# Moving both ends of on-chip memory: 256 bytes more at the left end, 384 more at the right end

## The chip, the cores and the metric

The kernel runs on one core of one Trainium2 chip. The metric is device time in microseconds (us) of one execution. A core has five engines that run their own instruction streams: TensorE (PE in the profile; its weight loads are listed apart as PEld), VectorE (DVE), ScalarE (ACT), GpSimd (POOL) and SyncE (SP, which here issues nearly all DMAs). They share the on-chip memory SBUF, 128 partitions wide; an address below is a byte address within a partition. TensorE reads two operands from it: the weights of a matmul (`lhsT`, 128 columns, loaded by an instruction of their own, LDWEIGHTS) and the moving operand (`rhs`, here mostly 512 columns of 4 bytes), and writes to PSUM.

## The reference, cut to what matters

One layer of a streaming encoder on x of shape (1, 2048, 1024), in float32:

```python
h = rmsnorm(x, mix_norm_g)
q, k, v, u, vg = split(h @ w_in)                 # 1024 -> 2560
a = band_attention(q, k, v, ...)                 # 8 heads x 64, chunks of 64, 8 chunks back
g = gelu(u) * spatial(rmsnorm(gelu(vg)))         # per group a 128x128 mix over positions
x = x + concat(rmsnorm(a), rmsnorm(g)) @ w_out   # 1024 -> 1024
h = rmsnorm(x, ffn_norm_g)
gate, up = split(h @ w_ffn_in)                   # 1024 -> 2 x 2816
x = x + (silu(gate) * up) @ w_ffn_out            # 2816 -> 1024
```

## The kernel before, in words

The large products keep float32 accuracy by splitting each operand into a rounded part (type float32r) and the rest; `split` (lines 80 to 82) makes them, ACT the first and DVE the second, and `mm3` (lines 84 to 87) runs three matmuls for one product: high times high, high times low, low times high. So lines 85, 86 and 87 carry nearly all TensorE work, in four stages:

1. Projections (`project`, line 272): 80 units of 8 x 3 matmuls of 128x512. `xh`, `xl` are the weights of the array (pool `xs`), `wh`, `wl` move (pool `ws`). Between them stand the small mix of the gating group (`pm`, line 329) and, in the second half, the attention of the first four tiles.
2. Attention of the other tiles (lines 160 to 210) with pieces of the output projection (`out_piece`, line 548) between the heads: one piece is one `mm3`, `mh`, `ml` as weights and `woh`, `wol` moving. The order of TensorE in this stage is written out by hand.
3. The first FFN product, by a seven-product scheme (Strassen-Winograd) on 2x2 blocks: `block` (line 715) runs seven products of 12 matmuls, 84 in all; 44 blocks, 22 in each half of the positions. Product number o reads the moving tiles `ys[o]` (made by `prep`, line 678, from `y_d`) and weights out of the pool `wi3` (made by `weights`, line 691). Line 671 puts the pools of `ys[5]` and `ys[6]` on the right side of memory; `ys[0]` to `ys[4]` are on the left.
4. The second FFN product, by the same scheme (`product`, line 803): 77 groups of 8 x 3 matmuls, `ah`, `al` (pool `at4`) as weights and `oh`, `ol` (pool `wt4`) moving.

Outside stage 2 a planner orders the instructions by a simulated time. Each engine then runs its list in order and waits on semaphores.

Memory is handed out from two ends. A pool on the left side starts where the pools below it end, a pool on the right side ends where those above it start, so the size of the first tile at an end moves every pool of that side. On the left come 16384 bytes that the runtime keeps, 128 bytes of built-in constants and the pool `consts` (line 46: `ident` and `identr` 512 bytes each, `nhalf` and `g1` 32, `rx` 64); the next pool starts at byte 17664. On the right, under the top of memory at 229376, come 32 bytes and the tile `edge` (line 48: 24 floats, 96 bytes), which nothing uses; the pool below ends at 229248. With the sizes of the pools between, the tiles that TensorE reads start at these addresses modulo 512 (each tile or slice that a 128x512 matmul reads is a multiple of 512 bytes from the next):

| stage | weights | side, mod 512 | moving | side, mod 512 |
|---|---|---|---|---|
| 1 | `xh`, `xl` | right, 0 | `wh`, `wl` | right, 0 |
| 1, mix | `wsh`, `wsl` | left, 288 | `vh`, `vl`, four strided slices of 64 | left, 256 or 0 |
| 2 | `mh`, `ml` | left, 256 | `woh`, `wol` | left, 256 |
| 2 | `qd` | right, 128 | `kTw` | right, 128 and 384 |
| 2, transposes | `pr` | right, 384 | `ident` | left, 128 |
| 3 | `wih`, `wil` | right, 384 | `ys[0]` to `ys[4]` | left, 256 |
| 3 | `wih`, `wil` | right, 384 | `ys[5]`, `ys[6]` | right, 384 |
| 4 | `ah`, `al` | left, 256 | `oh`, `ol` | right, 384 |

Of the kernel before, what the change touches and what calls it, by code (L numbers as in the profile page):

```python
# [8 lines left out]
F32 = mybir.dt.float32  # L9
# [9 lines left out]
P = 128  # L19
# [23 lines left out]
def block_kernel(ctx: ExitStack, tc: tile.TileContext, x, xT, w_in, mixg, qg, kg, bias, sgug, wsT, bsp, outg, w_out, ffng, w_fi, w_fo, out):  # L43
    nc = tc.nc

    consts = ctx.enter_context(tc.tile_pool(name="consts", bufs=1))
    edge = ctx.enter_context(tc.tile_pool(name="edge", bufs=1, side="right"))
    edge.tile([P, 24], F32, name="edge")
    dram = ctx.enter_context(tc.tile_pool(name="dram", bufs=1, space=DRAM))

    kT_d = dram.tile([P, H, SEQ], F32, name="kT_d")
# [837 lines left out]
```

## Time and profile before

| | |
|---|---|
| median of 3 runs | 2252.26 us (2251.11 to 2253.65) |
| profiled execution | 2248.34 us, its span 2246.6 us |
| granted clock of TensorE, mean | 0.998 |
| PE busy | 2200.9 us, 98% |
| PEld busy | 1810.0 us, 81% |
| DVE, ACT, POOL busy | 56%, 41%, 41% |
| DMA queue q1, share of 16 engines | 48.0% |

Rows below come from one profiled execution. The span runs from its first to its last instruction. A matmul's record lasts longer than the distance to the next start, since matmuls are pipelined: the rate is read from the starts, or from the number of records in a stretch, not from the duration. A `bank<-yh,wih` is a matmul into the PSUM tile `bank` from the tiles `yh` and `wih`.

### The profile page before, as it was taken

Reading aid. Unit: us, or ns where it says so; the run is one execution under the profiler, and the core shown is the slowest. Engines: PE = TensorE matmul, PEld = TensorE weight load, DVE = VectorE, ACT = ScalarE, POOL = GpSimd, SP = SyncE. Lnnn points to the kernel's source line nnn. Section 1 sums busy time; section 2 is a strip of 40 time slices with the busy share of each in tenths; the row PEclk is TensorE's granted clock in tenths of the full one; section 3 lists DMA queues with packets and bytes.
Section 4 is the critical chain, followed back from the end, with each engine's and each line's share of the span. In section 5 each row is a group of like instructions: output and inputs, shape, how many; then the busy total and the mean of one; then the engine's idle time right before and its main releaser. Section 6 shows DMA issues by size and latency. Waiting matters only on the chain.

```text
span 2246.6 us, 33040 instructions
## 1 busy us (share of the span) xinstructions
PE 2200.9 (98%) x12648; PEld 1810.0 (81%) x12648; DVE 1268.4 (56%) x1799; ACT 911.8 (41%) x1663; POOL 915.8 (41%) x789
## 2 busy tenths in 40 slices
PE   8999999999999999799999998999999999999999
PEld 7888888887888888688888886788888878888787
DVE  3366345774666666775555558565555533544555
ACT  6434544554555555443333335333332323222322
POOL 1254114320011100756566665665656412603434
PEclk9999999999999999999999999999999999999999
DMA  7244616558878873932323236232323263733463
GB/s 259 76 131 135 221 66 191 166 168 295 252 226 265 265 234 131 298 118 90 122 89 120 82 131 194 89 121 89 113 89 113 95 234 134 283 117 119 151 229 133
DMA packets 183805, 361.37 MB, mean 161 GB/s; under 512 B 15328, under 2 KB 68576, under 8 KB 182112
## 3 DMA queue, kind: packets, MB, share of 16 engines
q1 hardware_dynamic: 183504, 359.27, 48.0%
q8 instruction: 99, 1.62, 0.3%
q14 instruction: 58, 0.48, 0.1%
q10 hardware_dynamic: 144, 0.00, 0.0%
HBM read 256.45 MB, written 102.76 MB: 160 GB/s over the span
## 4 chain that ended last, share of the span: by engine, by line
PE 82%; DVE 4%; POOL 4%; DMA 4%; issue 3%; ACT 2%; SPq 1%; POOLq 0%; DVEq 0%; ACTq 0%
PE bank L85 17%; PE bank L86 17%; PE bank L87 17%; PE ps L85 6%; PE ps L86 6%; PE ps L87 6%; PE pv L210 2%; PE S L171 2%; PE pt L198 2%; PE po L85 2%; PE po L87 2%; PE po L86 2%; DMA kTw<-kT_d 1%; DMA ynat<-y_d 1%; POOL g L723 1%
## 5 line engine op out<-in xcount | busy, mean ns | idle before, releaser
L86 PE MATMUL bank<-yl,wih 128*128 128x512 f32 x1232 | 486.5, 395 | 4.0 <-DVE yl L82 4.0
L85 PE MATMUL bank<-yh,wih 128*128 128x512 f32 x1232 | 483.4, 395 | 7.0 <-ACT wih L81 5.0
L87 PE MATMUL bank<-yh,wil 128*128 128x512 f32 x1232 | 482.4, 394 | 0.0
L85 PEld LDWEIGHTS bank<-yh,wih 128*128 128x128 f32 x1232 | 232.2, 189 | 63.5 <-ACT wih L81 5.4
L86 PEld LDWEIGHTS bank<-yl,wih 128*128 128x128 f32 x1232 | 232.1, 188 | 60.7 <-DVE yl L82 7.1
L87 PEld LDWEIGHTS bank<-yh,wil 128*128 128x128 f32 x1232 | 232.0, 188 | 53.8
L85 PE MATMUL ps<-wh,xh 128*128 128x512 f32 x640 | 251.7, 398 | 7.9 <-ACT wh L81 7.9
L86 PE MATMUL ps<-wl,xh 128*128 128x512 f32 x640 | 250.2, 392 | 1.7 <-DVE wl L82 1.7
L87 PE MATMUL ps<-wh,xl 128*128 128x512 f32 x640 | 250.4, 391 | 0.0
L86 PE MATMUL bank<-ol,ah 128*128 128x512 f32 x616 | 243.1, 395 | 0.0
L85 PE MATMUL bank<-oh,ah 128*128 128x512 f32 x616 | 240.8, 395 | 1.0 <-ACT oh L81 1.0
L82 DVE TENSOR_TENSOR al<-ar,ah 128x1024 fp32r<-128x1024 f32 x77 | 109.5, 1421 | 212.8 <-ACT ah L81 212.7
L87 PE MATMUL bank<-oh,al 128*128 128x512 f32 x616 | 224.5, 395 | 1.7 <-DVE al L82 1.7
L82 DVE TENSOR_TENSOR wil<-s,wih 128x512 fp32r<-128x512 f32 x176 | 172.6, 1013 | 76.5 <-ACT wih L81 76.3
L81 ACT CAST ah<-ar 128x1024 fp32r<-128x1024 f32 x77 | 80.8, 1049 | 301.7 <-PE bank L86 281.2
L723 POOL TENSOR_TENSOR g<-up,g 128x512 f32<-128x512 f32 x88 | 138.6, 1576 | 82.2 <-DVE up L722 82.2
L81 ACT CAST wih<-s 128x512 fp32r<-128x512 f32 x176 | 101.5, 617 | 169.2 <-POOL s L700 116.1
L85 PEld LDWEIGHTS ps<-wh,xh 128*128 128x128 f32 x640 | 120.6, 189 | 31.0 <-ACT wh L81 7.9
L81 ACT CAST wih<-wir 128x512 fp32r<-128x512 f32 x132 | 81.5, 617 | 157.7 <-PE bank L86 144.9
L86 PEld LDWEIGHTS ps<-wl,xh 128*128 128x128 f32 x640 | 120.6, 188 | 25.9 <-DVE wl L82 2.5
L87 PEld LDWEIGHTS ps<-wh,xl 128*128 128x128 f32 x640 | 120.4, 188 | 25.0
L87 PEld LDWEIGHTS bank<-oh,al 128*128 128x128 f32 x616 | 116.0, 188 | 29.2 <-DVE al L82 2.2
(175 smaller groups left out, 4092.7 us busy)
## 6 DMA issues: line engine op xcount, KB each, us to landing
wir<-in_w_fi SPq DMA_DIRECT2D x88, 512.0 KB, 3.3
ar<-f_d SPq DMA_DIRECT2D x77, 512.0 KB, 3.3
kTw<-kT_d SPq DMA_DIRECT2D x96, 320.0 KB, 4.1
f_d<-g SPq DMA_DIRECT2D x22, 1024.0 KB, 4.2
wr<-in_w_in SPq DMA_DIRECT2D x40, 512.0 KB, 5.0
f_d<-c SPq DMA_DIRECT2D x22, 768.0 KB, 4.5
wor<-in_w_fo SPq DMA_DIRECT2D x66, 256.0 KB, 3.7
ynat<-y_d SPq DMA_DIRECT2D x56, 256.0 KB, 4.6
```

The costliest lines, as they stand in the source:

```text
L81: nc.scalar.copy(hi, src)
L82: nc.vector.tensor_sub(lo, src, hi.bitcast(F32))
L85: nc.tensor.matmul(ps, lhsT=lh, rhs=rh, start=first, stop=False)
L86: nc.tensor.matmul(ps, lhsT=lh, rhs=rl, start=False, stop=False)
L87: nc.tensor.matmul(ps, lhsT=ll, rhs=rh, start=False, stop=last)
L171: nc.tensor.matmul(S[:, i, :hw], lhsT=q[:, p], rhs=k[:, i * hw : (i + 1) * hw], start=p == 0, stop=p == 1)
L198: nc.tensor.transpose(pt[:, i], pr[:, i * P : (i + 1) * P], ident)
L210: nc.tensor.matmul(o, lhsT=a[:, i], rhs=vt[m + 1 - nk + i][:, c, h * HD : (h + 1) * HD], start=n == 0, stop=n == len(seq) - 1)
L723: nc.gpsimd.tensor_tensor(g[:, i], t, g[:, i], op=ALU.mult)
```

## The change

The tile `edge` at the right end grows from 24 to 120 floats (96 to 480 bytes), and a tile `skip` of 64 floats (256 bytes) is added to the pool `consts`, ahead of `ident`. Nothing reads or writes either. All tiles behind `skip` on the left lie 256 bytes higher, all pools on the right 384 bytes lower; with the 32 bytes above it `edge` now fills 512 bytes, and the left pools start at byte 17920, which is 35 x 512.

```diff
     consts = ctx.enter_context(tc.tile_pool(name="consts", bufs=1))
     edge = ctx.enter_context(tc.tile_pool(name="edge", bufs=1, side="right"))
-    edge.tile([P, 24], F32, name="edge")
+    edge.tile([P, 120], F32, name="edge")
+    consts.tile([P, 64], F32, name="skip")
     dram = ctx.enter_context(tc.tile_pool(name="dram", bufs=1, space=DRAM))
```

## Rows read from the trace of the kernel before

**Rows 1.** The page: busy us of each engine; the chain's shares by engine.

```profile
PE 2200.9 (98%) x12648; PEld 1810.0 (81%) x12648; DVE 1268.4 (56%) x1799; ACT 911.8 (41%) x1663; POOL 915.8 (41%) x789
...
PE 82%; DVE 4%; POOL 4%; DMA 4%; issue 3%; ACT 2%; SPq 1%; POOLq 0%; DVEq 0%; ACTq 0%
```

**Rows 2.** Windows by stage: us; PE, PEld, DVE, ACT, POOL busy (count); clock; DMA.

```profile
0.00:630.00 630.00, 612.49 (x3864) 513.81 (x3865) 346.33 (x591) 315.82 (x599) 158.65 (x244) 1.00 0.56 180
...
929.00:1803.40 874.40, 858.74 (x3681) 692.34 (x3681) 513.35 (x617) 307.02 (x513) 544.37 (x372) 0.99 0.34 118
1803.40:2241.60 438.20, 435.46 (x1873) 352.35 (x1871) 212.93 (x203) 126.34 (x166) 158.13 (x102) 1.00 0.49 173
```

**Rows 3.** Windows, PE alone, tile ps (projections): us, busy (count), clock, DMA.

```profile
215.00:315.00 100.00, 100.00 (x443) 1.00 0.46 163
```

**Rows 4.** Windows, PE alone, tile bank: the two FFN stages.

```profile
1095.00:1365.00 270.00, 270.00 (x1167) 1.00 0.33 113
...
1860.00:2120.00 260.00, 260.00 (x1121) 1.00 0.45 158
```

**Rows 5.** Groups by line and form, 1095:1365 and 1860:2120: busy, mean | idle, releaser.

```profile
L81 ACT CAST wih<-wir 128x512 fp32r<-128x512 f32 x42 | 25.9, 618 | 55.6 <-PE bank L86 55.6
...
L81 ACT CAST ah<-ar 128x1024 fp32r<-128x1024 f32 x47 | 49.3, 1049 | 179.8 <-PE bank L86 167.6 <-DMA ar<-f_d 11.3 <-PE bank L87 0.9
```

**Rows 6.** Timeline of PE in one block of stage 3: start us, us, what.

```profile
1178.08 0.40 PE L87 MATMUL bank<-yh,wil 128*128 128x512 f32 x1
...
1188.12 0.39 PE L85 MATMUL bank<-yh,wih 128*128 128x512 f32 x1
...
1190.91 0.39 PE L85 MATMUL bank<-yh,wih 128*128 128x512 f32 x1
...
1193.18 0.39 PE L86 MATMUL bank<-yl,wih 128*128 128x512 f32 x1
```

**Rows 7.** Timeline of PE: output projection at the end of stage 2.

```profile
917.50 0.39 PE L86 MATMUL po<-wol,mh 128*128 128x512 f32 x1
...
925.20 0.39 PE L87 MATMUL po<-woh,ml 128*128 128x512 f32 x1
```

**Rows 8.** Windows, PE alone: the two long stretches of stage 3.

```profile
953.00:1323.80 370.80, 370.80 (x1601) 1.00 0.30 105
...
1437.30:1803.40 366.10, 366.07 (x1580) 1.00 0.29 105
```

**Rows 9.** Chain of waits, change of halves, first and last: start us, us, what.

```profile
1323.85 0.69 DVE u L737
...
1437.33 0.50 PE bank L85
```

**Rows 10.** Chain of waits at the start of stage 3.

```profile
947.19 1.94 PE pth L572 x8
...
950.64 0.43 PE bank L85
```

**Rows 11.** Timeline of PE in stage 2: a piece's end, then a transpose.

```profile
682.23 0.39 PE L87 MATMUL po<-woh,ml 128*128 128x512 f32 x1
682.46 0.27 PE L195 MATMUL S<-ident,pr 128*128 128x128 f32 x1
```

**Rows 12.** Groups by line and form, 1095:1365: POOL.

```profile
L723 POOL TENSOR_TENSOR g<-up,g 128x512 f32<-128x512 f32 x27 | 42.5, 1576 | 22.5 <-DVE up L722 22.5
...
L735 POOL TENSOR_TENSOR v<-v,u 128x512 f32<-128x512 f32 x14 | 22.1, 1576 | 11.6 <-ACT v L734 11.6
```

**Rows 13.** The page's DMA issues: out<-in, count, KB each, us to landing.

```profile
wir<-in_w_fi SPq DMA_DIRECT2D x88, 512.0 KB, 3.3
ar<-f_d SPq DMA_DIRECT2D x77, 512.0 KB, 3.3
```

**Rows 14.** Timeline of PE: the gating group's mix in stage 1.

```profile
83.49 0.28 PE L86 MATMUL pm<-vl,wsh 128*128 128x256 f32 x1
...
84.32 0.28 PE L87 MATMUL pm<-vh,wsl 128*128 128x256 f32 x1
```

## The prediction

> **What bounds the kernel now.** I read the busy line first: TensorE is busy 98% of the span, no other engine above 56%, and the chain that ended last lies on PE for 82% [rows 1]. A busy PE may still run below its own best rate, so the stages come next, by the windows [rows 2]: the projections (0 to 630 us), the FFN's first products (929 to 1803) and its second ones (1803 to 2242); the attention with the output projection lies between 630 and 929. PE is busy 97 to 99% of the three, so the time of a stage is its number of matmuls times the distance between two starts. That distance is what I compare from stage to stage. A window counts each record that overlaps it; a 512-column record lasts 0.39 to 0.40 us and starts are 0.23 us apart, so 1.7 of the count began before the window.
>
> Projections: 100 us with 443 - 1.7 records, 226.6 ns from start to start [rows 3]. First FFN products: 270 / (1167 - 1.7) = 231.7 ns; second ones: 260 / (1121 - 1.7) = 232.3 ns [rows 4]. All three run at granted clock 1.00 and with no PE idle time, with the same shape and type. The slower two aren't short of operands either: the casts that make them, on ACT, wait for PE to give buffers back (55.6 of 55.6 us for `wih<-wir`, 167.6 of 179.8 for `ah<-ar`) [rows 5].
>
> What differs is where the operands lie. By the table of residues in the section on the kernel before, `ws` and `xs` agree modulo 512 (both 0), `oh` and `ah` don't (384, 256), and in the first FFN products two of seven pairs agree: `ys[5]` and `ys[6]`, on the right like the weights at 384; `ys[0]` to `ys[4]` are at 256. One block of 84 matmuls shows both: from 1178.08 us 43 starts take 10.04 us, 233.5 ns each, in the products with `ys[1]` to `ys[4]`; at its end, in those with the right-hand tiles, ten starts take 2.27 us, 227 ns [rows 6]. Output projections at the end of the attention, left with left, both 256: 34 starts in 7.70 us, 226.5 ns [rows 7]. So pairs at 0/0, 256/256 and 384/384 run at 226.5 to 227 ns (I take 226.7), pairs that differ by 128 or 384 at about 232 to 233.
>
> **The change part by part.** No instruction is added or removed; two tiles that nobody uses move every other address. Left tiles go up by 256 bytes, right ones down by 384, which is +128 modulo 512.
>
> Second FFN products: 256 and 384 both become 0. 616 x 3 = 1848 matmuls x (232.3 - 226.7) = 10.3 us. PE is on the chain there throughout, and ACT and DVE wait for it.
>
> First FFN products: 256 + 256 and 384 + 128 both become 0, so the five unmatched pairs match and the two matched ones stay so. The saving is 231.7 - 226.7 = 5.0 ns per matmul, averaged over the seven products, but only where PE sets the time. From 953 to 1323.8 us and from 1437.3 to 1803.4 us it does: 1601 + 1580 - 3.4 = 3178 matmuls [rows 8], 15.9 us. Between the two, as the halves change, the chain runs for 113 us through DVE, POOL and the loads of `ynat`, and comes back to PE at 1437.33 [rows 9]; a faster PE waits longer there, and I count nothing. At the start the chain runs through the transposes that wait for `h` until 947 us [rows 10]; nothing there either.
>
> Projections: 0/0 become 128/128. No row has a 512-column pair at 128. The bound from one side is nothing, from the other the price of an unmatched pair, 640 x 3 x 5.0 = 9.6 us. The nearest rows are the three equal pairs, all alike, so I take nothing.
>
> Attention: `woh` and `mh` stay equal, and `kTw` and `qd` both move by 128. What changes is the neighbour across the sides: where a right-hand weight load runs behind an output projection, as at 682.23 us, the spacing is 230 ns here [rows 11]. 256 + 256 + 256 such matmuls x up to 5 ns make -3.8 to +3.8 us; a gain is likelier, since the first transposes' weights (384 against 256) would then agree with `woh`. I take 0.5 us.
>
> Other engines: POOL's product of a left and a right tile (256, 384; L723) takes 1576 ns, that of two left ones (256, 256; L735) 1576 ns [rows 12], so agreement is worth nothing to it. DMA: `wir` lands at residue 384, `ar` at 256, both 512 KB in 3.3 us [rows 13]. Nothing again; the bound is the landing time of a few loads at the change of halves, 1 us either way. [...]
>
> Sum: 10.3 + 15.9 + 0.5 = 26.7 us, of which I take 26, since the first groups of a stage lag. Against the profiled execution (2248.34 us: the span of 2246.6 and 1.7 around it) that is 2222. The median of the runs shown is 3.9 us above that execution, so I set it against the median: 2252.3 - 26 = 2226 us.
>
> [...] Matched matmuls run at 226.7 ns here [rows 3, 7]. [...]
>
> **The rivals.** *Sides, not residues: no change.* Every matched 512-column pair in the trace also lies on one side of memory, and nearly every slow one has an operand on each. If the side decides, moving both ends does nothing: 2252 us. For it: no row shows a pair across the sides at equal residue. Against it: the mix `pm`, left with left at 288 against 256 or 0, takes 0.83 us for 7 matmuls of 256 columns, 118.6 ns [rows 14], where half of 226.7 is 113.4; but its moving operand is strided, so this is weak. [...] Chance 0.07.
>
> *Slower: the side decides, and the projections fall out of step.* Then the FFN gains nothing, and the pair at 128/128 is not like 0/0; at the unmatched price the projections pay 1920 x 5.0 = 9.6 us: 2262 us. It decides as soon as more than about 5 us is lost there without the FFN's gain. For it: 128 is the one residue that no row shows for a 512-column pair. Against it: 0, 256 and 384 alike. Chance 0.05.
>
> *Part of it.* If the other stage boundaries swallow more (PE ahead of the weights' preparation, the projections losing their 9.6 us while the FFN gains), 10 to 17 us remain: 2235 to 2242 us. Against it: ACT waits for PE in both FFN stages [rows 5]. Chance 0.10.
>
> **How the numbers follow.** Forecast 0.78: 2220 to 2232 us, from 20 to 32 us saved (26, with 3.8 of the attention and 2 of the clock either way). With the near half of the third rival the range is 2219 to 2237 us. About 0.2% (4.5 us) is what a measurement of this kernel can tell from no change. Faster: 0.78 + 0.10 = 0.88; the same 0.07; slower 0.05.
>
> **What would show it.** In the changed kernel the same windows should count: first FFN products 270 / 0.2267 + 1.7 = 1193 records in 270 us for 1167, second ones 1149 in 260 us for 1121, projections still 443 in 100 us. All seven products of a block should show 227 ns, a block 84 x 226.7 ns = 19.04 us for 84 x 231.7 = 19.46. The 113 us at the change of halves should stay as long, with up to 2 us more of waiting in it. The prediction is wrong if the FFN windows still count 1167 and 1121 (the sides decide), or if the projections' count falls.

## The result and the profile after

The changed kernel takes 2228.53 us (median of 4 runs, 2227.2 to 2230.03) against 2252.22 us of the kernel before on the same chip (4 runs): a ratio of 0.9895 [0.9878, 0.9912], 23.7 us less. Two more sets of the same kernel gave 0.9896 and 0.9901 (below). The forecast was 2226 us in a range of 2219 to 2237.

The profiled execution took 2228.25 us, its span 2226.5. It holds the same 12648 matmuls in the same order; the line numbers are one higher (L86 to L88 are `mm3`). First the page of the changed kernel, the lines that answer to [rows 1]:

```profile
PE 2177.4 (98%) x12648; PEld 1811.7 (81%) x12648; DVE 1277.8 (57%) x1799; ACT 911.2 (41%) x1663; POOL 910.6 (41%) x789
...
PE 79%; DMA 5%; DVE 5%; POOL 4%; issue 4%; ACT 2%; SPq 1%; DVEq 0%; POOLq 0%; ACTq 0%
```

PE's busy time falls by 23.5 us and its share of the span stays at 98%: the engine that set the time still does, and does the same list faster. Where, the windows by stage tell (columns as in [rows 2]; stages 1 and 2 in one):

```profile
0.00:934.40 934.40, 909.84 (x7096) 768.39 (x7097) 542.11 (x980) 478.54 (x985) 211.81 (x315) 1.00 0.61 194
934.40:1793.10 858.70, 842.45 (x3681) 692.23 (x3680) 520.46 (x617) 306.17 (x513) 542.25 (x372) 0.99 0.35 120
1793.10:2221.80 428.70, 425.06 (x1873) 351.05 (x1871) 214.35 (x204) 126.54 (x166) 156.53 (x102) 1.00 0.51 177
```

Stage 3 takes 858.7 us for 874.4, stage 4 428.7 for 438.2, with the same counts of matmuls. Stages 1 and 2 end at 934.4 for 929: 5.4 us later in this execution, which comes back below. The spacing within the two FFN stages, PE alone, tile `bank`, answers to [rows 4]:

```profile
1095.00:1365.00 270.00, 270.00 (x1193) 1.00 0.34 117
1860.00:2080.00 220.00, 220.00 (x972) 1.00 0.48 166
```

270 / (1193 - 1.7) = 226.6 ns for 231.7, and 220 / (972 - 1.7) = 226.7 ns for 232.3: 26 more matmuls in the same 270 us, at the same granted clock and with PE never idle. The timeline of PE in one block of stage 3, in the products with left-hand tiles that ran at 233.5 ns in [rows 6]:

```profile
1180.20 0.39 PE L87 MATMUL bank<-yl,wih 128*128 128x512 f32 x1
...
1185.64 0.39 PE L87 MATMUL bank<-yl,wih 128*128 128x512 f32 x1
```

24 starts in 5.44 us, 226.7 ns: as fast as the right-hand tiles were before. A whole block takes 19.04 us for 19.45. The projections' window, tile `ps`, answers to [rows 3]:

```profile
215.00:315.00 100.00, 99.71 (x440) 1.00 0.48 167
```

440 records for 443, in 0.3 us less of busy time; from start to start 226.9 ns for 226.7: the pair at 128/128 runs as the one at 0/0 did. The 5.4 us of stages 1 and 2 show in the waits of PE before 934.4 us (us in total, times, longest), of which the first two are absent before:

```profile
PE Ss L179 <- DMA qe<-qe_d: 2.7, 1, 2.7
PE S L172 <- DMA kTw<-kT_d: 2.5, 1, 2.5
```

Two loads of the attention came late, and behind the wait for `qe` the granted clock was 0.57 from 368 to 372 us. In two other executions with the same addresses stage 3 begins at 929.64 and 930.11 us, so the 5.4 us are not lost in every execution. But a wait for one of these loads or for both, of 0.4 to 2.8 us each, stands in all 13 profiles with moved addresses and not in the one before. Whether the moved addresses have a share in it stays open, with one profile of before.

### The profile page after: what moved, and what is told of

Its sections match the earlier page's. It is cut to its first block, busy times and chain, and to the rows that moved or that the text cites. A ratio compares the mean times of both kernels' runs of the same rounds, so it can differ in the third digit from the quotient of the medians.

```text
span 2226.5 us, 33040 instructions
## 1 busy us (share of the span) xinstructions
PE 2177.4 (98%) x12648; PEld 1811.7 (81%) x12648; DVE 1277.8 (57%) x1799; ACT 911.2 (41%) x1663; POOL 910.6 (41%) x789
## 4 chain that ended last, share of the span: by engine, by line
PE 79%; DMA 5%; DVE 5%; POOL 4%; issue 4%; ACT 2%; SPq 1%; DVEq 0%; POOLq 0%; ACTq 0%
PE bank L86 16%; PE bank L88 16%; PE bank L87 16%; PE ps L86 5%; PE ps L87 5%; PE ps L88 5%; PE pv L211 2%; PE S L172 2%; PE pt L199 2%; PE po L86 2%; PE po L87 2%; PE po L88 2%; DMA kTw<-kT_d 1%; DVE wil L83 1%; POOL g L724 1%
## 5 line engine op out<-in xcount | busy, mean ns | idle before, releaser
L86 PE MATMUL bank<-yh,wih 128*128 128x512 f32 x1232 | 478.8, 391 | 7.7 <-DVE g L719 3.1
L87 PE MATMUL bank<-yl,wih 128*128 128x512 f32 x1232 | 481.8, 391 | 4.0 <-DVE yl L83 3.9
L88 PE MATMUL bank<-yh,wil 128*128 128x512 f32 x1232 | 477.5, 390 | 0.0
L86 PEld LDWEIGHTS bank<-yh,wih 128*128 128x128 f32 x1232 | 232.1, 188 | 59.1 <-DVE g L719 4.6
L87 PEld LDWEIGHTS bank<-yl,wih 128*128 128x128 f32 x1232 | 232.1, 188 | 55.1 <-DVE yl L83 7.3
L88 PEld LDWEIGHTS bank<-yh,wil 128*128 128x128 f32 x1232 | 232.2, 188 | 48.2
L86 PE MATMUL ps<-wh,xh 128*128 128x512 f32 x640 | 252.9, 400 | 7.8 <-ACT wh L82 7.8
L87 PE MATMUL ps<-wl,xh 128*128 128x512 f32 x640 | 251.5, 394 | 1.7 <-DVE wl L83 1.7
L88 PE MATMUL ps<-wh,xl 128*128 128x512 f32 x640 | 252.0, 394 | 0.0
L87 PE MATMUL bank<-ol,ah 128*128 128x512 f32 x616 | 239.8, 389 | 0.0
L86 PE MATMUL bank<-oh,ah 128*128 128x512 f32 x616 | 237.5, 389 | 1.6 <-ACT oh L82 1.6
L83 DVE TENSOR_TENSOR wil<-s,wih 128x512 fp32r<-128x512 f32 x176 | 177.8, 1048 | 85.8 <-ACT wih L82 85.7
L88 PE MATMUL bank<-oh,al 128*128 128x512 f32 x616 | 221.2, 389 | 2.1 <-DVE al L83 2.1
L86 PEld LDWEIGHTS ps<-wh,xh 128*128 128x128 f32 x640 | 121.3, 190 | 31.0 <-ACT wh L82 7.8
L87 PEld LDWEIGHTS ps<-wl,xh 128*128 128x128 f32 x640 | 121.4, 190 | 26.0 <-DVE wl L83 2.6
L88 PEld LDWEIGHTS ps<-wh,xl 128*128 128x128 f32 x640 | 121.2, 189 | 25.2
L700 POOL TENSOR_TENSOR s<-wir 128x512 f32<-128x512 f32 x44 | 59.9, 1360 | 189.8 <-DMA wir<-in_w_fi 179.9
```

What stands on the lines that cost most here:

```text
L83: nc.vector.tensor_sub(lo, src, hi.bitcast(F32))
L86: nc.tensor.matmul(ps, lhsT=lh, rhs=rh, start=first, stop=False)
L87: nc.tensor.matmul(ps, lhsT=lh, rhs=rl, start=False, stop=False)
L88: nc.tensor.matmul(ps, lhsT=ll, rhs=rh, start=False, stop=last)
L700: nc.gpsimd.tensor_add(s1, x21, x22)
```

## The experiments

Unless a diff says otherwise, an experiment starts from the changed kernel. "Difference" is the byte address of the moving operand less that of the weights, modulo 512.

**One end, by 128 bytes.** The left end moves by 128, the right stays as before. All FFN pairs then agree at 384/384, none at 0.

```diff
-    edge.tile([P, 120], F32, name="edge")
-    consts.tile([P, 64], F32, name="skip")
+    edge.tile([P, 24], F32, name="edge")
+    consts.tile([P, 32], F32, name="skip")
```

> The change with one end alone and without a multiple of 512: the left end moves up by 128 bytes, the right end stays. Left tiles come to 384 modulo 512, as the right ones of both FFN stages are; the projections keep 0/0. Theory (the pair must agree modulo 512): stage 3 counts 1192 records of tile bank in 270 us (226.7 ns), a block takes 19.04 us, stage 4 1148 in 260 us; time 2226 to 2231 us, as the changed kernel or up to 2 us below it. Rival A (both operands must lie at multiples of 512): 231.7 and 232.3 ns as before, 2250 to 2254 us. Rival B (the sides decide): the same 2250 to 2254 us.

2231.86 us against 2255.09, ratio 0.9903 [0.9888, 0.9918]; block 19.04 us. Agreement decides, not the residue of zero, and not the side: left tiles against right weights take 227.0 ns (1189 records of `bank` in 269.52 busy us from 1095 to 1365, clock 1.00), where they took 231.7. Padding to multiples of 512 wasn't needed. The time is 0.9 us over the range expected for it.

**The changed kernel again**, beside it on the same chip.

> The changed kernel once more, unaltered. Theory (the 5 us that stages 1 and 2 took longer in its first profile are loads that land late, by chance): stages 1 and 2 end within 3 us of the 929 us of before, the FFN stages again at 19.04 us a block and 5.44 us a group; time 2227 to 2230 us. Rival (the new residues slow the loads of qe and kTw): waits of 2 to 3 us for qe and kTw and the clock's fall near 368 us stand in this profile too, stage 3 starts at 933 us or later.

2230.59 us, ratio 0.9896 [0.9880, 0.9913], from which the first experiment cannot be told. Its stage 3 begins at 929.64 us, as expected; the waits for `kTw` and `qe` stand here too, at 1.6 and 0.8 us.

**The right end alone.** Left stays at 256, right goes to 0: every pair across the sides differs by 256.

```diff
-    consts.tile([P, 64], F32, name="skip")
```

> The right end's part of the change alone: right tiles at 0 in both FFN stages, left tiles stay at 256, the projections at 128/128. The pairs of ys[0] to ys[4] and of stage 4 now differ by 256. Theory (agreement modulo 512): they run slow, at 229 to 236 ns, time 2245 to 2256 us. Rival (the period is 256 bytes): 226.7 ns everywhere in stages 3 and 4, time 2226 to 2231 us.

2232.48 us, ratio 0.9902 [0.9883, 0.9921]: as fast as with both ends within the intervals, though 1.5 us over the rival's range. The window of PE, tile `bank`:

```profile
1095.00:1365.00 270.00, 269.94 (x1192) 1.00 0.34 118
```

226.8 ns at a difference of 256. I had expected such pairs to be slow; the account by 512 bytes missed. A difference of 256 is as good as none, so the right half of the change alone does it. The left half alone was not run; it would set 0 against 384 in the FFN stages, which still differ by 128 modulo 256.

**Two scans of the difference.** Unused tiles between the pools of `ys[0]` to `ys[4]` give each product of a block its own difference; the tiles are renamed, so that the trace tells them apart. The second scan has the paddings 96, 64, 32, 128 and 128.

```diff
+PADS = (32, 32, 64, 128, 256)
...
+            n = PADS[i]
+            if n:
+                pool(st, f"pad{i}", 1).tile([P, n // 4], F32, name=f"pad{i}")
```

> The changed kernel with unused tiles between the left pools of stage 3, so that the moving tiles yh_a to yh_e lie 32, 64, 128, 256 and 0 bytes above the weights modulo 512, yh_f and yh_g at 0; nothing else differs. Theory (any difference modulo 512 costs): a to d at 230 to 236 ns per matmul, e to g at 227 ns; a block at 19.2 to 19.4 us. Rival (only the 64-byte, 128-byte or 256-byte period matters): the products above that period at 227 ns too (period 64: b, c, d; period 128: c, d; period 256: d). One look, no verdict of time: about 2228 to 2245 us.

> As the first scan, with yh_a to yh_e 96, 160, 192, 320 and 448 bytes above the weights modulo 512, yh_f and yh_g at 0. Theory (period 256): all five above 227 ns, d (320) as 64 was, 229 to 230 ns, and c (192) like e (448). Rival (period 512 with a second zero at 256): d differs from what 64 showed, c from e. One look; about 2238 to 2250 us.

Timeline of PE in one block of the first scan, each row the first matmul of its product but the first row, which is the fourth; the letters a to f stand for differences of 32, 64, 128, 256, 0 and (on the right) 0:

```profile
1180.68 0.39 PE L87 MATMUL bank<-yh_a,wih 128*128 128x512 f32 x1
...
1182.78 0.39 PE L87 MATMUL bank<-yh_b,wih 128*128 128x512 f32 x1
...
1185.52 0.39 PE L87 MATMUL bank<-yh_c,wih 128*128 128x512 f32 x1
...
1188.31 0.39 PE L87 MATMUL bank<-yh_d,wih 128*128 128x512 f32 x1
...
1191.03 0.39 PE L87 MATMUL bank<-yh_e,wih 128*128 128x512 f32 x1
...
1193.75 0.39 PE L87 MATMUL bank<-yh_f,wih 128*128 128x512 f32 x1
```

Nine starts in 2.10 us at 32 (233 ns), then twelve in 2.74 (228), 2.79 (232.5), 2.72 and 2.72 (226.7 both). The same in the second scan, from c on for 192, 320, 448 and 0, with the next product's start as the last row:

```profile
1184.38 0.39 PE L87 MATMUL bank<-yh_c,wih 128*128 128x512 f32 x1
...
1187.17 0.39 PE L87 MATMUL bank<-yh_d,wih 128*128 128x512 f32 x1
...
1189.93 0.39 PE L87 MATMUL bank<-yh_e,wih 128*128 128x512 f32 x1
...
1192.71 0.39 PE L87 MATMUL bank<-yh_f,wih 128*128 128x512 f32 x1
...
1195.48 0.40 PE L87 MATMUL bank<-yh_a,wih 128*128 128x512 f32 x1
```

Mean distances of starts within a product, from 1095 to 1320 us, in ns by the difference: 32, 233.8; 64, 229.1; 96, 235.1; 128, 231.7; 160, 233.2; 192, 232.9; 256, 227.0; 320, 229.4; 448, 233.1. 320 repeats 64 and 448 repeats 192, and 256 is free after its first matmul (231 ns behind the product at 128, then 226 to 227): a period of 256. None of the tested differences between multiples is free, but the price isn't the same for all. One run each: 2241.11 and 2242.96 us.

The price also reaches past the pair that disagrees. Products at difference 0 run at 226.7 ns throughout in the first scan where one at 256 or 0 stands before them (e, f). Product f of the second scan, at 0 but behind one at 448, takes 230.8 ns in the rows above and 230.5 on the mean, and comes back to 227 only with its last two matmuls. Product g, at 0 behind one that disagrees, takes 228.9 and 229.5 ns in the two scans. And at a single difference the matmuls need not pay alike: in the kernel before, at 384, every second start came some 237 to 239 ns behind the last one, the others some 228 to 230. So a price belongs to a run of matmuls, not to one pair; and 384 there took 233.7 ns on the mean, for 231.7 at 128 here, which by the period alone would be alike.

**The cost put into another stage.** 128 bytes between the pools of the projections' moving operand and weights:

```diff
-        sm, tmp, ws, xs = (pool(st, n, b, "right") for n, b in (("sm1", 4), ("tmp1", 2), ("ws", 4), ("xs", 4)))
+        sm, tmp, ws, gap, xs = (
+            pool(st, n, b, "right") for n, b in (("sm1", 4), ("tmp1", 2), ("ws", 4), ("gap", 1), ("xs", 4)))
+        gap.tile([P, 32], F32, name="gap")
```

> The changed kernel with an unused tile of 128 bytes between the pools ws and xs, so that the projections, which have agreed in every kernel so far, disagree by 128 (weights at 0, moving at 128 modulo 512); stages 3 and 4 stay as changed. Theory (disagreement costs by itself, wherever it is): stage 1 goes from 227 to about 232 ns, 1920 x 5 = 9.6 us, stage 3 starts 8 to 11 us later, time 2236 to 2242 us. Rival (the gain of stages 3 and 4 has another cause, in what those stages hold): stage 1 stays at 227 ns, time 2226 to 2232 us.

2237.62 us, ratio 0.9917 [0.9898, 0.9936]; its window of PE, tile `ps`:

```profile
215.00:315.00 100.00, 99.52 (x429) 1.00 0.49 168
```

By starts this is 232.6 ns for the 226.9 of the changed kernel, and over all of the stage 232.5 for 227.5 (starts less than 260 ns apart); 1920 x 5.0 ns are 9.6. Stage 3 begins at 939.72 us, some 10 later than at 929.64 and 930.11. The interval of the ratio overlaps those of the changed kernel, so the windows carry this, not the total. Here both operands lie on the right and still disagree: the side plays no part by itself.

**Which weights must agree?** A weight load's record starts 2 to 5 ns behind the start of the matmul before its own and lasts 188 ns, and a matmul's record lasts 389 ns, so three partners were possible: the matmul's own weights, the next ones, the next but one. Gaps of 128 bytes inside the pools put the low tiles `yl` and `wil` at a difference of 128 to the high ones; a second tile of 128 bytes behind each keeps everything else as it is modulo 256.

```diff
                 yh = yp[o].tile([P, 4, 512], F32R, tag="yh", name=f"yh{hf}{o}")
+                if hf == 0:
+                    yp[o].tile([P, 32], F32, tag="gap", name="gap")
...
                 h = wi.tile([P, 4, P], F32R, tag="wih", name="wih")
+                if not gaps:
+                    gaps.append(wi.tile([P, 32], F32, tag="gap", name="gap", bufs=1))
...
```

> The changed kernel with the low halves of stage 3 moved by 128 bytes: yl and wil come to 128 modulo 256, yh and wih stay at 0. Per product step the three matmuls are yh with wih, yl with wih, yh with wil. Theory N (a moving operand must agree modulo 256 with the weights that are loaded behind it while it streams: yh with wih, yl with wil, yh with wih): every such pair still agrees, a block takes 19.04 us, time 2226 to 2232 us. Rival O (it must agree with the weights that it is multiplied with): lines 87 and 88 disagree, 56 of 84 matmuls pay 5 to 7 ns, a block takes 19.3 to 19.4 us, time 2237 to 2243 us.

2242.08 us, ratio 0.9945 [0.9924, 0.9967]; mean block 19.42 us, 0.37 more than in the changed kernel (19.045), as 56 x 6.6 ns would be. Were the next weights alone the partner, each `yl` would have met `wil` and nothing been lost; that theory fell. Then the same with the second and third matmul of a step exchanged, `wih` by `yh`, `wil` by `yh`, `wih` by `yl`:

```diff
-                mm3(bk, w[0][:, k], w[1][:, k], y[0][:, k], y[1][:, k], k == 0, k == 3)
+                nc.tensor.matmul(bk, lhsT=w[0][:, k], rhs=y[0][:, k], start=k == 0, stop=False)
+                nc.tensor.matmul(bk, lhsT=w[1][:, k], rhs=y[0][:, k], start=False, stop=False)
+                nc.tensor.matmul(bk, lhsT=w[0][:, k], rhs=y[1][:, k], start=False, stop=k == 3)
```

> The kernel of the pair experiment (yl and wil at 128, yh and wih at 0 modulo 256) with the last two matmuls of each product step exchanged: yh with wih, yh with wil, yl with wih. Rival O (a moving operand must agree with the weights that it is multiplied with): still two of three disagree, a block at 19.4 us as there. Theory P (it must agree with the weights loaded two matmuls ahead, which are read while its columns really stream): yh meets wih, yh meets wih, yl meets wil; all agree, a block at 19.04 us, stage 3 at 227 ns.

One run, 2244.09 us; mean block 19.40 us, 0.35 more. The next but one alone fell too (it would have paid nothing). Two halves of the pair's diff were left, `yl` alone and `wil` alone:

> The changed kernel with only the low moving tiles yl of stage 3 at 128 modulo 256; wih, wil and yh stay at 0. One moving operand in three (line 87) disagrees with all weights around it. Rival O (the pair that is multiplied must agree) and theory B (a moving operand must agree with both weight loads that run while it streams, those one and two matmuls ahead) say the same: 28 of 84 matmuls pay some 7 ns, a block at about 19.2 us.

> The changed kernel with only the low weights wil of stage 3 at 128 modulo 256; wih, yh and yl stay at 0. Rival O: only line 88 (yh with wil) disagrees, 28 of 84, a block at about 19.2 us as with yl alone. Theory B: wil is loaded one ahead of line 87's end and two ahead of line 86's, so the streams of lines 86 and 87 disagree with a load beside them, 56 of 84, a block at about 19.4 us. Should a block stay at 19.04 us, neither holds.

One run each: 2234.71 and 2244.92 us, and mean blocks of 19.23 and 19.42 us: 0.18 and 0.375 more, as 28 x 6.5 and 56 x 6.7 ns would be. Since a price can reach past its pair, the sums don't tell which matmuls pay; the lines do. Shortest, median and longest record in ns by line, 1095 to 1320 us, of `yl` alone:

```profile
L86 PE MATMUL bank<-yh,wih x328: 388/389/398, 1094.7 to 1319.4; 128*128 128x512 f32 x164
L87 PE MATMUL bank<-yl,wih x328: 390/395/395, 1095.0 to 1319.6; 128*128 128x512 f32 x164
```

and of `wil` alone:

```profile
L87 PE MATMUL bank<-yl,wih x325: 389/396/396, 1094.6 to 1319.3; 128*128 128x512 f32 x163
L88 PE MATMUL bank<-yh,wil x325: 395/397/404, 1094.8 to 1319.6; 128*128 128x512 f32 x163
L86 PE MATMUL bank<-yh,wih x325: 389/389/396, 1095.1 to 1319.8; 128*128 128x512 f32 x163
```

In the changed kernel all three medians are 389. By starts it is the same: with `yl` moved, the next start comes 234.1 ns behind L87 and 226 to 227 behind the other two; with `wil` moved, 232.4 behind L87, 234.3 behind L88 and 226.9 behind L86. So with `wil` moved L87 pays, though its own weights `wih` agree with it: the matmul's own weights alone don't explain it, nor does a price that reaches over from L88, since L86 between the two pays nothing. L88 pays too, whose next and next but one loads (`wih`) agree with it, and L86 doesn't, whose next but one is `wil`: theory B had the number of matmuls right (56) and the lines wrong. "Own and next" names the right lines in both runs, and in the exchanged pair too, where it has all three pay: they do, by 3 to 5 ns each on the mean. In the pair it has L86 free, and there the next start comes 236 or 224 ns behind L86 in turn, 230.2 on the mean; and why the blocks of the exchanged pair alternate between 19.24 and 19.56 us it doesn't tell. Shown is that the matmul's own weights aren't all that counts, nor the next ones alone, nor the next but one alone. That own and next are the two is likely, not settled.

**Transposes and the mix.** `ident` (128) and `wsh`, `wsl` (32) moved to 0 modulo 256, without moving any other pair's agreement. (`identr`, which the expectation names too, lay at 0 modulo 256 already.)

```diff
-    consts.tile([P, 64], F32, name="skip")
+    consts.tile([P, 32], F32, name="skip")
...
+    consts.tile([P, 32], F32, name="skip2")
...
+        c1.tile([P, 56], F32, name="skip3")
         wsh = c1.tile([P, G, P], F32R, name="wsh")
```

> The changed kernel, and the pairs that it leaves apart brought together too: ident and identr, which move in every transpose, go from 128 to 0 modulo 256 (the skip tile is cut in two halves around them), and the weights wsh and wsl of the gating group's mix from 32 to 0. Theory (every moving operand that disagrees with the weight loads beside it pays some 7 ns): the mix falls from 119 to about 114 ns for 256 columns, 0.5 us in all; the 944 transposes of 128 columns pay at most 7 ns each, so stages 1 and 2 end 0.5 to 7 us earlier, time 2222 to 2230 us. Rival (transposes are bound by something else at 109 ns): nothing but the mix changes, 2228 to 2231 us.

2231.26 us, ratio 0.9894 [0.9874, 0.9914]. The mix takes 119.8 ns from start to start (distances under 200 ns), 118.2 without the edit; the transposes of the probabilities stay at a median of 109 ns. Nothing was gained, against the expectation: the rule holds for the 128x512 matmuls tested, and did not show in these shorter or strided ones.

**The changed kernel a third time**, beside it.

> The changed kernel unaltered, beside the version with aligned transposes on the same chip: 2227 to 2232 us, transposes at 109 ns from start to start, the mix at 119 ns.

2232.62 us, ratio 0.9901 [0.9883, 0.9920], 0.6 us over the range expected; stage 3 begins at 930.11 us. No version beats the change by more than the intervals allow.

## Why the prediction was right

*Second FFN products: 10.3 us forecast, 9.5 measured* (438.2 to 428.7). The spacing came out as taken, 226.7 ns; PE's waits in this stage, for `oh` and `al`, grew from 2.7 to 3.7 us, about what is missing. In the two other profiles of the same kernel the stage is 432.4 and 432.8 us long, so it gained 6 only: PE waits 4.1 and 5.4 us there, and behind such a wait, at some 1808 or 1811 us and once at 2108, matmuls start 0.43 us apart for a while (mean granted clock 0.79 and 0.82 from 1806 to 1814 us, and once 0.91 from 2104 to 2124, for 1.00 before). The profile of before has no such stretch in this stage. Whether the change makes them more frequent stays open: there is one profile of before to set against them.

*First FFN products: 15.9 us forecast, 15.7 measured*, but not all from where it was forecast. The blocks of the two stretches where PE sets the time (2 to 22 and 26 to 44) gained 14.2 us: among them stands a new wait of PE for `g` of 1.4 us, at some 1041 us. The first block, for which nothing was counted, gained 1.8: behind its first wait eight starts of before come 0.43 us apart (granted clock 0.50 from 947 to 952 us), one of after (0.64 from 951 to 955, 0.92 from 955 to 958). The three blocks at the change of halves take 26.8, 20.8 and 21.1 us for 26.8, 20.9 and 20.8, in sum 0.2 more: faster matmuls wait longer there, as forecast. That the two errors cancelled is luck; in the two other profiles of the same kernel the stage gained 15.3 and 12.4 us. No run shows the 2 us that the forecast's range took for the clock either way: over the three blocks at the change of halves the mean granted clock was 0.95 for 0.98, and they took the 0.2 us more.

*Projections: 0 forecast, and 0* (440 and 441 records in two executions, for 443 [rows 3]); the gap put between their pools (232.5 ns) shows that the other bound, 9.6 us, was a real one.

*Attention: 0.5 us forecast, not seen.* Output projections run at 232.0 ns on the mean, 232.2 before (distances under 300 ns): the term was within its bounds of 3.8 us and nearest to nothing. *Other engines and the DMA: nothing forecast.* POOL's and DVE's busy times move by under 1%; of the DMA, the late loads of the attention stay open, as said.

The two FFN stages add up to 25.2 us, and the two profiled executions are 20.1 apart, since stages 1 and 2 took 5.4 back; between the medians it is 23.7. In the two other profiles the FFN stages gain some 21 and 18 us against the one profile of before, which is of an execution 3.9 us faster than its median.

The rivals by sides fell to the first experiment and to the gap in the projections. The runs differ, 226.7 against up to 235.1 ns for one shape by addresses alone.

Three steps of the reasoning were right in outcome only. "Modulo 512" was too coarse: the residues of the 512-column pairs in the table (0, 256 and 384) are multiples of 128, and before the change a difference of 256 occurred in no 512-column pair, and the trace could not tell 256 from 512. And the mix at 288 against 256 or 0 [rows 14] was taken as evidence against the sides; the mix showed no gain when its weights were aligned, so it was none. And the price was taken to belong to a pair: the ten starts at 227 ns [rows 6] leave out the first matmuls of their product, which still cost 231 to 232 ns behind the unmatched one, so that the matched products ran at 228.0 on the mean. None of this altered the sum, because the same pairs matched by either period, and because it took the mean of all seven products, 231.7 ns, to 226.7 for all.

## What to carry to other kernels

Where PE is 98% busy and two stages with matmuls of one shape and clock differ in spacing, compare the operands' addresses before looking for a wait: here all tested differences that are not multiples of 256 bytes cost 2 to 8 ns in 227. One unused tile at one end of memory is enough to test it (here 128 bytes took stage 3 from 231.7 to 227.0 ns), and a second run with the misalignment put into another stage shows that it is the cause (here 226.9 to 232.6 ns in the projections). Which instructions pay is read by line or by product, not from a sum that a number of matmuls happens to fit. Count records in windows rather than read the page's mean durations, which show it less plainly (395 to 391 ns), and credit the gain only to stretches where that engine sets the time, less the waits that a faster engine meets (here PE's waits in stage 4 grew from 2.7 to 3.7 us, and stage 3 had a new one of 1.4 us).

## What the runs showed of the hardware that was not expected

- Over the differences tested the price repeated after 256 bytes (differences of 256 and 0: 227.0 and 226.7 ns; 64 and 320: 229.1 and 229.4; 192 and 448: 232.9 and 233.1).
- The price is not the same at all differences: 229.1 ns at 64, 233.8 at 32, 235.1 at 96, and 232.9 at 192 though it is as far from a multiple as 64. Nor is it the same at one difference in all places (231.7 at 128 in the scan, 232.3 in stage 4 before [rows 4]). No run explains this.
- The price reaches past the pair: a product at difference 0 behind one at 448 took 230.5 ns on the mean, and was back at 227 with its last two matmuls only.
- Not only the matmul's own weights count: with `wil` alone moved, `yl` on `wih` pays (396 ns for 389), though the two agree.
- Agreeing pairs of 512 columns ran at 226.5 to 227.0 ns on the mean, and at up to 230.5 behind a product that disagreed; what sets these numbers was not tested.
